# Joined 512-column matmuls in the Strassen-like gate/up products, taken apart into 256-column matmuls with one PSUM bank per product

## The chip, the cores and the metric

One core of one Trainium2 chip runs the whole kernel. The metric is the device time of one launch in microseconds (us), as the median of a few runs.

## The reference, cut to what matters

Two layers of an encoder block over 512 tokens of width 1024. The change touches only the gate and up products of the two feed-forward blocks of each layer (four in all):

```
def swiglu(x, w_gate, w_up, w_down):          # D_MODEL 1024, D_FF 2816, SEQ 512
    return (jax.nn.silu(x @ w_gate) * (x @ w_up)) @ w_down

for l in range(DEPTH):                         # DEPTH 2
    x = x + 0.5 * swiglu(rms_norm(x, ffn1_norm[l]), ...)
    ...                                        # attention and convolution, untouched
    x = x + 0.5 * swiglu(rms_norm(x, ffn2_norm[l]), ...)
    x = rms_norm(x, post_norm[l])
```

All of it is float32. The kernel reaches that accuracy by splitting each operand into a high part `hi` (rounded to the type fp32r) and a low part `lo` (what the rounding left), and by adding three matmuls: high weights by high data, high weights by low data, low weights by high data. The helper `mm3` issues these three, at L194, L195 and L196.

## The kernel before, in words

The 2816 hidden columns are worked in four chunks. The first chunk uses plain products on all 512 tokens (512-column matmuls through `mm3`). The other three chunks take two 128-column groups of gate and up together as a **pair** (nine pairs in each feed-forward, 36 in all) and use a Strassen-like scheme: features and tokens are cut in halves, and seven half-size products replace eight. A product works on 256 tokens (`HS`) and four 128x128 weight blocks for gate and four for up.

In the function `pair` the seven products run on TensorE in this order, kept by `order["pe"]`: b11, b21, t2, t3, t1, t4, b22. Four of them (b11, t2, t1, b22) go through `product`: 2 x 4 x 3 matmuls of 256 columns into one PSUM bank `bx`, gate in its left half and up in its right. Three (b21, t3, t4) go through `product_joined`: high and low data of a block lie side by side in one tile (`xj`, 512 columns), so that one 512-column matmul with the high weights does hi\*hi and hi\*lo at once (L418), and one 256-column matmul adds the low weights (L419):

```
T.matmul(o, w[0][:, c], both, start=start and k == 0, stop=False, skip_group_check=True)
last = T.matmul(o[:, 0:HS], w[1][:, c], both[:, 0:HS], start=False, stop=k == 3, ...).ins
```

A joined product therefore needs a bank for gate and one for up, each with the main sum on the left and the hi\*lo part on the right. VectorE (DVE) and ScalarE (ACT) add the two parts when they take the result out: `by` by two additions for each bank (L459, L460), `bz` after t3 by a copy for each bank (L428) and an addition of the halves (L470), `bz` after t4 by L477 and L478.

Weights come by DMA as float32 quarters (`fr`, `raw` tiles). DVE forms their sums for the scheme (L453 to L456), ACT casts the high part into a ring of four slots (`weights`, L284 and L442), and DVE subtracts for the low part (L286). For b21 and t4 the low part is made by an ACT pass (L434) and an accumulating DMA from GpSimd's queue into `ls` (L435). The slots lie at offsets `WOFF` and the tiles are padded by small gap tiles, so that the addresses of weights and data keep a fixed relation.

After a pair, `split` (L201, L202) makes high and low parts of its results. After the second and the third chunk `down` does the second matrix product in the same scheme, on 256-column matmuls through `mm3`, with the three pairs of the chunk as its inner dimension; its first products need the split results of the last pair. The order on each engine is fixed when the kernel is built: a scheduler places the instructions, bound by the `issue_after` rules in the code.

Of the kernel before, what the change touches and what calls it, by code (L numbers as in the profile page):

```python
# [62 lines left out]
WOP = 4  # L63
EVP = "DAD"
ORDER = "t0s1p3v4o5"
JOINED = ("b21", "t3", "t4")

VECS = [("g1", 8), ("gm", 8), ("g2", 8), ("gp", 8), ("gql", 3), ("gkl", 2),
        ("cw", 4 * CK), ("cb", 4), ("lg", 4), ("lb", 4), ("gq", 1), ("gk", 1), ("cp", PT)]
# [12 lines left out]
def encoder_kernel(ctx: ExitStack, tc: tile.TileContext, xT, consts, vecs, rgain, wgu1, wd1, wdq1,  # L82
# [210 lines left out]
    def ffn_body(fpool, l, gx, norm, wgu, wd, wdq, gain, done, w0, halved):  # L293
# [56 lines left out]

        def operands(R):

            def joined(src):
                both = fpool.tile([P, 2, S], FR, tag="xj", name=nm("xj"), bufs=WIDE)
                A.copy(both[:, :, 0:HS], src)
                V.tensor_tensor(both[:, :, HS:S], src, both[:, :, 0:HS].bitcast(FP), ALU.subtract)
                return both

            def halved(src, own=False):
                hi, lo = (fpool.tile([P, S], FR, tag="xs", name=nm("xs"), bufs=2) if own else slot(FR)  # L360
                          for _ in range(2))
                h3, l3 = (v.rearrange("p (j t) -> p j t", j=2) for v in (hi, lo))
                A.copy(h3, src)
                V.tensor_tensor(l3, src, h3.bitcast(FP), ALU.subtract)
                return hi, lo

            def diff(a, b, op=ALU.subtract):
                t = tmp().rearrange("p (j t) -> p j t", j=2)
                V.tensor_tensor(t, a, b, op)
                return t  # L370
            for i in range(2):
                e, o = wide(quarter()), wide(quarter())
                for j in range(2):
                    for par, t in ((0, e), (1, o)):
                        m = 4 * i + 2 * j + par
                        V.scalar_tensor_tensor(t[:, j], x[:, m, :], gain[:, m:m + 1], R, ALU.mult, ALU.mult)
                        yield
                b11, b12, b21, b22 = (v[:, :, h * HS:(h + 1) * HS] for v in (e, o) for h in range(2))
                for n, src in (("b11", b11), ("b21", b21)):
                    X[n].append((joined if n in JOINED else halved)(src))  # L380
                    yield
                t3 = diff(b12, b22)
                yield
                t2 = diff(t3, b11)
                yield
                X["t2"].append((joined if "t2" in JOINED else halved)(t2))
                yield
                X["t3"].append((joined if "t3" in JOINED else halved)(t3))
                yield
                t1 = diff(b11, b12)  # L390
                yield
                X["t1"].append((joined if "t1" in JOINED else halved)(t1))
                yield
                t4 = diff(b21, t2, ALU.add)
                yield
                X["t4"].append((joined if "t4" in JOINED else halved)(t4))
                yield
                X["b22"].append(halved(b22, i == 1))
                yield

        def product(o, w, n, start, stop):
# [6 lines left out]
                        last = mm3(o[:, gu * HS:(gu + 1) * HS], w[0][:, c], w[1][:, c], hi[:, t], lo[:, t],  # L408
                                   start and gu == 0 and k == 0, stop and k == 3, True)
            order["pe"] = last  # L410

        def product_joined(os, w, n, start):
            with tc.issue_after(order["pe"]):
                for gu, o in enumerate(os):
                    for k in range(4):
                        both = X[n][k // 2][:, k % 2]
                        c = slice(gu * 512 + k * P, gu * 512 + (k + 1) * P)
                        T.matmul(o, w[0][:, c], both, start=start and k == 0, stop=False, skip_group_check=True)  # L418
                        last = T.matmul(o[:, 0:HS], w[1][:, c], both[:, 0:HS], start=False, stop=k == 3,  # L419
                                        skip_group_check=True).ins  # L420
            order["pe"] = last

        def parts(os):

            return [(slice(gu * HS, (gu + 1) * HS), o[:, 0:HS], o[:, HS:S]) for gu, o in enumerate(os)]

        def copied(o, src):
            A.copy(o, src)  # L428
# [9 lines left out]
        def summed(w, src, n=WC, lo=None):  # L438

            lo = subtracted(w, src, n) if lo is None else lo  # L440
            hi = part(0, True)
            in_turn("h", lambda: A.copy(hi[:, :n], src[:, :n]))  # L442
            return hi, lo

        def pair(p, quartered):

            a11, a12, a21, a22, s3 = quarters(wgu[l, p], WC, p == CHUNKS[0][1])
            bx, by, bz = bank(), (bank(), bank()), (bank(), bank())
            product(bx, split_into("a11", a11), "b11", True, True)
            a = copied(tmp(), bx)  # L450
            product_joined(by, summed(wgu[l, p, 1], a12), "b21", True)
            with after("first"):
                V.tensor_tensor(s3, a11, a21, ALU.add)  # L453
                V.tensor_tensor(a21, a21, a22, ALU.add)
                V.tensor_tensor(a11, a11, a21, ALU.add)  # L455
                V.tensor_tensor(a12, a12, a11, ALU.add)  # L456
            s = tmp()
            for c, main, rest in parts(by):
                V.tensor_tensor(a[:, c], a[:, c], main, ALU.add)  # L459
                V.tensor_tensor(a[:, c], a[:, c], rest, ALU.add)  # L460
                if c.start == 0:
                    A.activation(s[:, 0:HS], a[:, 0:HS], AF.Silu)
            V.tensor_tensor(s[:, 0:HS], s[:, 0:HS], a[:, HS:S], ALU.mult)
            product(bx, split_into("s2", a11), "t2", False, True)
            r2 = wide(fpool.tile([P, WC], FP, tag="e", name=nm("e"), bufs=1))
            copied(r2[:, 0], bx)
            product_joined(bz, split_into("s3", s3), "t3", True)
            d = [copied(tmp(), o) for o in bz]
            for t in d:
                V.tensor_tensor(t[:, 0:HS], t[:, 0:HS], t[:, HS:S], ALU.add)  # L470
            product(bx, split_into("s1", a21), "t1", False, True)
            copied(r2[:, 1], bx)
            for t, (c, _, _) in zip(d, parts(bz)):
                order["first"] = V.tensor_tensor(r2[:, 1, c], t[:, 0:HS], r2[:, 1, c], ALU.subtract).ins
            product_joined(bz, summed(wgu[l, p, 3], a22), "t4", False)
            for c, main, rest in parts(bz):
                V.tensor_tensor(r2[:, 0, c], main, r2[:, 0, c], ALU.subtract)  # L477
                V.tensor_tensor(r2[:, 0, c], rest, r2[:, 0, c], ALU.add)  # L478
            s2 = tmp()
            s2v = s2.rearrange("p (h t) -> p h t", h=2)  # L480
            A.activation(s2v, r2[:, :, 0:HS], AF.Silu)
            V.tensor_tensor(s2v, s2v, r2[:, :, HS:S], ALU.mult)
# [12 lines left out]
            order["u0"] = V.tensor_tensor(u[:, h1], u[:, h0], s[:, h0], ALU.subtract).ins  # L495
            V.tensor_tensor(v[:, h0], s[:, h0], s[:, h1], ALU.subtract)
# [829 lines left out]
```

## Time and profile before

| what | before |
|---|---|
| median of 3 runs | 1773.75 us (1773.36 to 1775.32) |
| the profiled execution, its own time | 1775.6 us |
| its span, first to last instruction | 1773.8 us |
| TensorE (PE) busy, matmuls | 1757.2 us, 11430 |
| weight loads (PEld) busy | 1555.0 us, 11430 |
| DVE busy, instructions | 1488.6 us, 2309 |
| ACT busy, instructions | 1095.9 us, 1699 |
| GpSimd (POOL) busy | 381.3 us |
| mean granted TensorE clock | 1.000 |

PE is busy in 99% of the span, so what counts is how fast one matmul follows another. The durations of single matmuls overlap (they are pipelined); the distance from the start of one to the start of the next is read from the timeline, and is called the pace below. A pair takes about 19.5 us, the three pairs of the second feed-forward's third chunk run from 706 to 764.7 us of the span, and the `down` behind them from 764.7 to 794.7 us.

### The profile page before, as it was taken

To read this page: it belongs to the slowest core of one execution; us is meant where nothing else is said; L and a number is where in the kernel's file an instruction comes from. 1 tells how busy PE (TensorE), PEld (TensorE's weight loads), DVE (VectorE), ACT (ScalarE), POOL (GpSimd) and SP (SyncE) were. 2 spreads that over 40 slices of the span, in tenths; PEclk is the share of its full clock that TensorE was granted. 3 is DMA by queue.
4 is the path that set the end of the run, shared out by engine and by line. 5 is a ranking of instruction groups with operands and counts; after the bars stand their busy time and mean duration, and the time that the engine had idled before them with its cause. 6 is when DMAs were issued, how large, how long until landed. Compare 5 with 4: busy or idle time off the path is not lost. (4 is left out here: it accounts for less than half of the span.)

```text
span 1773.8 us, 29449 instructions
## 1 busy us (share of the span) xinstructions
PE 1757.2 (99%) x11430; PEld 1555.0 (88%) x11430; DVE 1488.6 (84%) x2309; ACT 1095.9 (62%) x1699; POOL 381.3 (21%) x315
## 2 busy tenths in 40 slices
PE   9999999999999999999999999999999999999998
PEld 7899999888678899999888999998986788999997
DVE  7899988688965999998779989885989568999883
ACT  5576766467953575756645757564778435767664
POOL 1001010248823000000310000002576410000001
PEclk9999999999999999999999999999999999999999
DMA  5567565324303466665326575743251126575742
GB/s 181 146 149 180 142 173 122 120 79 122 80 25 101 113 165 164 153 170 141 115 75 162 131 194 128 194 119 113 78 150 34 58 79 155 140 183 138 188 109 81
DMA packets 71947, 228.28 MB, mean 129 GB/s; under 512 B 8448, under 2 KB 9600, under 8 KB 71808
## 3 DMA queue, kind: packets, MB, share of 16 engines
q1 hardware_dynamic: 55536, 171.87, 30.7%
q0 software_dynamic: 16128, 54.53, 18.3%
q8 instruction: 89, 1.46, 0.3%
q14 instruction: 50, 0.41, 0.1%
q10 hardware_dynamic: 144, 0.00, 0.0%
HBM read 222.19 MB, written 2.10 MB: 126 GB/s over the span
## 5 line engine op out<-in xcount | busy, mean ns | idle before, releaser
L194 PE MATMUL ps<-r,weights 128*128 128x256 f32 (+1 forms) x2556 | 804.6, 318 | 2.8 <-ACT weights L1142 1.4
L195 PE MATMUL ps<-r,weights 128*128 128x256 f32 (+1 forms) x2556 | 804.4, 315 | 1.3 <-DVE r L202 1.3
L196 PE MATMUL ps<-r,weights 128*128 128x256 f32 (+1 forms) x2364 | 750.2, 319 | 3.2 <-DVE weights L162 2.3
L194 PEld LDWEIGHTS ps<-r,weights 128*128 128x128 f32 x2556 | 480.0, 188 | 50.2 <-ACT t L428 4.5
L195 PEld LDWEIGHTS ps<-r,weights 128*128 128x128 f32 x2556 | 480.6, 188 | 37.7 <-DVE r L202 2.8
L196 PEld LDWEIGHTS ps<-r,weights 128*128 128x128 f32 x2364 | 444.0, 188 | 39.4 <-DVE weights L162 3.6
L418 PE MATMUL ps<-xj,weights 128*128 128x512 f32 x864 | 306.4, 395 | 0.0
L155 ACT CAST weights<-raw 128x1024 fp32r<-128x1024 f32 (+3 forms) x148 | 131.7, 902 | 213.6 <-PE ps L195 120.7
L284 ACT CAST weights<-fr 128x1024 fp32r<-128x1024 f32 (+1 forms) x160 | 157.3, 983 | 100.3 <-DVE fr L455 51.8
L435 POOL DMA_DIRECT2D ls<-in_wgu x72 | 62.7, 871 | 724.9 <-ACT ls L434 664.3
L162 DVE TENSOR_TENSOR weights<-raw,weights 128x1024 fp32r<-128x1024 f32 (+3 forms) x132 | 142.8, 1090 | 81.0 <-ACT weights L155 79.9
L286 DVE TENSOR_TENSOR weights<-fr,weights 128x1024 fp32r<-128x1024 f32 (+1 forms) x160 | 182.3, 1139 | 21.3 <-ACT weights L284 21.3
L418 PEld LDWEIGHTS ps<-xj,weights 128*128 128x128 f32 x864 | 161.5, 188 | 31.0
L419 PE MATMUL ps<-xj,ls 128*128 128x256 f32 x576 | 162.5, 282 | 0.0
L1005 POOL TENSOR_TENSOR y<-y,pr 128x495 f32<-128x495 f32 (+29 forms) x90 | 118.8, 1323 | 46.2 <-ACT pr L1003 40.9
L284 ACT CAST weights<-raw 128x1024 fp32r<-128x1024 f32 (+1 forms) x100 | 97.8, 978 | 43.9 <-PE ps L195 22.9
L286 DVE TENSOR_TENSOR weights<-raw,weights 128x1024 fp32r<-128x1024 f32 (+1 forms) x100 | 113.5, 1135 | 11.4 <-ACT weights L284 10.9
L434 ACT ACTIVATE ls<-fr 128x1024 fp32r<-128x1024 f32 (+1 forms) x56 | 56.1, 1001 | 85.6 <-PE ps L419 46.1
L419 PEld LDWEIGHTS ps<-xj,ls 128*128 128x128 f32 x576 | 108.6, 189 | 0.0
L231 POOL TENSOR_TENSOR r<-r,t 128x512 f32<-128x512 f32 x45 | 74.0, 1654 | 132.2 <-ACT t L227 131.8
L999 DVE SCALAR_TENSOR_TENSOR cv<-m,vec,cv 128x511 f32<-128x511 f32 (+14 forms) x120 | 88.0, 733 | 4.0 <-ACT cv L995 2.4
L435 POOL DMA_DIRECT2D ls<-in_wdq x32 | 27.7, 865 | 258.2 <-ACT ls L434 258.2
(258 smaller groups left out, 2917.8 us busy)
## 6 DMA issues: line engine op xcount, KB each, us to landing
fr<-in_wgu SPq DMA_DIRECT2D x112, 512.0 KB, 4.2
ls<-in_wgu POOLq DMA_DIRECT2D x72, 512.0 KB, 7.2
raw<-in_wgu SPq DMA_DIRECT2D x62, 512.0 KB, 4.5
fr<-in_wdq SPq DMA_DIRECT2D x48, 384.0 KB, 4.5
ls<-in_wdq POOLq DMA_DIRECT2D x32, 384.0 KB, 4.9
raw<-in_wd SPq DMA_DIRECT2D x32, 384.0 KB, 3.2
raw<-in_wd SPq DMA_DIRECT2D x32, 256.0 KB, 2.8
raw<-in_wcv SPq DMA_DIRECT2D x16, 512.0 KB, 3.6
```

The lines of the kernel that those rows point to most:

```text
L155: order["cast"] = in_turn("h", lambda: A.copy(hi[:, :w], raw[:, :w]))
L162: in_turn(e, lambda: e.tensor_tensor(lo[:, :w], raw[:, :w], hi[:, :w].bitcast(FP), ALU.subtract))
L194: T.matmul(o, lh, rh, start=first, stop=False, skip_group_check=free)
L195: T.matmul(o, lh, rl, start=False, stop=False, skip_group_check=free)
L196: order["mm"] = T.matmul(o, ll, rh, start=False, stop=last, skip_group_check=free).ins
L284: in_turn("h", lambda: A.copy(hi[:, :w], src[:, :w]))
L286: order["lo"] = in_turn(V, lambda: V.tensor_tensor(lo[:, :w], src[:, :w], hi[:, :w].bitcast(FP), ALU.subtract))
L418: T.matmul(o, w[0][:, c], both, start=start and k == 0, stop=False, skip_group_check=True)
L419: last = T.matmul(o[:, 0:HS], w[1][:, c], both[:, 0:HS], start=False, stop=k == 3, skip_group_check=True).ins
L435: G.dma_start(out=lo[:, :n], in_=w, accum_op=ALU.add)
L999: V.scalar_tensor_tensor(acc[:, s:], u[c][:, :S - s], tap(k), acc[:, s:], ALU.mult, ALU.add)
L1005: order["conv"] = G.tensor_tensor(ys[c][:, s:], ys[c][:, s:], pr[:, s:], ALU.add).ins
```

## The change

`product_joined` and its helper `parts` go. All seven products now run through `product`: for each block hi\*hi, hi\*lo and lo\*hi, 256 columns each, into one bank. The tile `xj` stays where it was; its two halves now hold the high parts of two blocks and the low parts of the same two blocks. With one bank for each of b21 and t3/t4 a result is taken out by one instruction of 512 columns where there were two or four of 256.

```
-JOINED = ("b21", "t3", "t4")
+APART = ("b21", "t3", "t4")
...
-            def joined(src):
-                both = fpool.tile([P, 2, S], FR, tag="xj", name=nm("xj"), bufs=WIDE)
-                A.copy(both[:, :, 0:HS], src)
-                V.tensor_tensor(both[:, :, HS:S], src, both[:, :, 0:HS].bitcast(FP), ALU.subtract)
-                return both
...
+            def halved(src, where=""):
+                if where == "xj":
+                    both = fpool.tile([P, 2, S], FR, tag="xj", name=nm("xj"), bufs=WIDE)
+                    hi, lo = both[:, 0], both[:, 1]
...
-            bx, by, bz = bank(), (bank(), bank()), (bank(), bank())
+            bx, by, bz = bank(), bank(), bank()
...
-            product_joined(by, summed(wgu[l, p, 1], a12), "b21", True)
+            product(by, summed(wgu[l, p, 1], a12), "b21", True, True)
...
+            V.tensor_tensor(a, a, by, ALU.add)
             s = tmp()
-            for c, main, rest in parts(by):
-                V.tensor_tensor(a[:, c], a[:, c], main, ALU.add)
-                V.tensor_tensor(a[:, c], a[:, c], rest, ALU.add)
-                if c.start == 0:
-                    A.activation(s[:, 0:HS], a[:, 0:HS], AF.Silu)
+            A.activation(s[:, 0:HS], a[:, 0:HS], AF.Silu)
...
-            product_joined(bz, split_into("s3", s3), "t3", True)
-            d = [copied(tmp(), o) for o in bz]
-            for t in d:
-                V.tensor_tensor(t[:, 0:HS], t[:, 0:HS], t[:, HS:S], ALU.add)
+            product(bz, split_into("s3", s3), "t3", True, True)
+            d = copied(tmp(), bz)
...
-            for t, (c, _, _) in zip(d, parts(bz)):
-                order["first"] = V.tensor_tensor(r2[:, 1, c], t[:, 0:HS], r2[:, 1, c], ALU.subtract).ins
-            product_joined(bz, summed(wgu[l, p, 3], a22), "t4", False)
-            for c, main, rest in parts(bz):
-                V.tensor_tensor(r2[:, 0, c], main, r2[:, 0, c], ALU.subtract)
-                V.tensor_tensor(r2[:, 0, c], rest, r2[:, 0, c], ALU.add)
+            order["first"] = V.tensor_tensor(r2[:, 1], d, r2[:, 1], ALU.subtract).ins
+            product(bz, summed(wgu[l, p, 3], a22), "t4", False, True)
+            V.tensor_tensor(r2[:, 0], bz, r2[:, 0], ALU.subtract)
```

The changed file is shorter, so its lines have other numbers: what stood at L428, L434, L442, L453 to L456 stands 17 lines higher there (L411, L417, L425, L436 to L439), and what stood at L462, L481, L482, L484, L485, L490 to L497, L525, L536 and L537 stands 25 lines higher for L481 and behind it (L456, L457, L459, L460 and so on) and 20 higher for L462 (L442). L440 adds `by`, L451 and L453 are the two new subtractions. Lines up to L354 keep their numbers.

In the program as built GpSimd's and SyncE's instructions stand in the order of before, and TensorE's products do too. The scheduler moved instructions on DVE and ACT in the pairs. The first place is DVE from the end of t1 over the end of t4 into the next pair, in the first chunk of pairs; `ps` are PSUM banks, `e` holds the results of t1 and t2, `fr` and `raw` are weight quarters. Before:

```order
L477 TENSOR_TENSOR e_1027<-ps_940,e_1027 128x256
L474 TENSOR_TENSOR e_1027<-t_1047,e_1027 128x256
L474 TENSOR_TENSOR e_1027<-t_1049,e_1027 128x256
L453 TENSOR_TENSOR raw_1166<-fr_1158,fr_1160 128x1024
L478 TENSOR_TENSOR e_1027<-ps_940,e_1027 128x256
L477 TENSOR_TENSOR e_1027<-ps_941,e_1027 128x256
L454 TENSOR_TENSOR fr_1160<-fr_1160,fr_1161 128x1024
L478 TENSOR_TENSOR e_1027<-ps_941,e_1027 128x256
L455 TENSOR_TENSOR fr_1158<-fr_1158,fr_1160 128x1024
L485 TENSOR_TENSOR t_994<-t_994,ps_937 128x256
L482 TENSOR_TENSOR t_1106<-t_1106,e_1027 128x512
```

The same place in the changed kernel:

```order
L451 TENSOR_TENSOR e_1041<-t_1069,e_1041 128x512
L436 TENSOR_TENSOR raw_1188<-fr_1180,fr_1182 128x1024
L453 TENSOR_TENSOR e_1041<-ps_950,e_1041 128x512
L437 TENSOR_TENSOR fr_1182<-fr_1182,fr_1183 128x1024
L457 TENSOR_TENSOR t_1128<-t_1128,e_1041 128x512
L438 TENSOR_TENSOR fr_1180<-fr_1180,fr_1182 128x1024
L460 TENSOR_TENSOR t_1012<-t_1012,ps_948 128x256
L202 TENSOR_TENSOR r_1163<-t_1128,r_1162 128x512
```

Six small instructions became two, the product with Silu (L482, now L457) moved ahead of the weight sum for t2 (L455, now L438), and the low part of that result (L202) moved ahead of the last weight sum.

The second place is ACT over the same time, from the copy of t1's result to the copy of the next pair's b11 (`t_1198`, now `t_1218`), which frees the bank that t2 writes. Before:

```order
L428 COPY e_1027<-ps_937 128x512
L434 ACTIVATE ls_1312<-fr_1161 128x1024
L481 ACTIVATE t_1106<-e_1027 128x512
L484 ACTIVATE t_994<-ps_937 128x256
L284 CAST weights<-fr_1158 128x1024
L284 CAST weights<-raw_1166 128x1024
L284 CAST weights<-fr_1160 128x1024
L201 CAST r_1140<-t_1106 128x512
L428 COPY t_1198<-ps_1167 128x512
```

The same place in the changed kernel:

```order
L411 COPY e_1041<-ps_948 128x512
L417 ACTIVATE ls_1340<-fr_1183 128x1024
L456 ACTIVATE t_1128<-e_1041 128x512
L459 ACTIVATE t_1012<-ps_948 128x256
L201 CAST r_1162<-t_1128 128x512
L284 CAST weights<-fr_1180 128x1024
L284 CAST weights<-raw_1188 128x1024
L284 CAST weights<-fr_1182 128x1024
L411 COPY t_1218<-ps_1189 128x512
```

The cast L201 moved from behind the three weight casts to ahead of them; nothing stands any more between the last weight cast and the copy.

The third place is DVE from the last pair of that chunk into `down`, up to the low part of the pair's second result (L202). Before:

```order
L536 TENSOR_TENSOR fr_1390<-fr_1390,fr_1391 128x768
L478 TENSOR_TENSOR e_1257<-ps_1170,e_1257 128x256
L477 TENSOR_TENSOR e_1257<-ps_1171,e_1257 128x256
L537 TENSOR_TENSOR fr_1388<-fr_1388,fr_1390 128x768
L478 TENSOR_TENSOR e_1257<-ps_1171,e_1257 128x256
L485 TENSOR_TENSOR t_1224<-t_1224,ps_1167 128x256
L482 TENSOR_TENSOR t_1336<-t_1336,e_1257 128x512
L496 TENSOR_TENSOR t_1375<-t_1224 128x256
L286 TENSOR_TENSOR weights<-fr_1388,weights 128x768
L494 TENSOR_TENSOR u_1374<-t_1224,t_1336 128x256
L202 TENSOR_TENSOR r_1371<-t_1336,r_1370 128x512
```

The same place in the changed kernel:

```order
L511 TENSOR_TENSOR fr_1423<-fr_1423,fr_1424 128x768
L512 TENSOR_TENSOR fr_1421<-fr_1421,fr_1423 128x768
L453 TENSOR_TENSOR e_1282<-ps_1191,e_1282 128x512
L286 TENSOR_TENSOR weights<-fr_1421,weights 128x768
L457 TENSOR_TENSOR t_1369<-t_1369,e_1282 128x512
L460 TENSOR_TENSOR t_1253<-t_1253,ps_1189 128x256
L469 TENSOR_TENSOR u_1407<-t_1253,t_1369 128x256
L471 TENSOR_TENSOR t_1408<-t_1253 128x256
L202 TENSOR_TENSOR r_1404<-t_1369,r_1403 128x512
```

Both weight sums (L536, L537, now L511, L512) now stand ahead of the subtraction from t4's bank, and the low weights for t2 (L286) moved ahead of the product with Silu.

More of the change, by code (lines that the diff above doesn't have):

```diff
@@ L351, in operands @@
         def operands(R):
-            def joined(src):
-                both = fpool.tile([P, 2, S], FR, tag="xj", name=nm("xj"), bufs=WIDE)
-                A.copy(both[:, :, 0:HS], src)
-                V.tensor_tensor(both[:, :, HS:S], src, both[:, :, 0:HS].bitcast(FP), ALU.subtract)
-                return both
-            def halved(src, own=False):
-                hi, lo = (fpool.tile([P, S], FR, tag="xs", name=nm("xs"), bufs=2) if own else slot(FR)
-                          for _ in range(2))
+            def halved(src, where=""):
+                if where == "xj":
+                    both = fpool.tile([P, 2, S], FR, tag="xj", name=nm("xj"), bufs=WIDE)
+                    hi, lo = both[:, 0], both[:, 1]
+                else:
+                    hi, lo = (fpool.tile([P, S], FR, tag="xs", name=nm("xs"), bufs=2) if where else slot(FR)
+                              for _ in range(2))
                 h3, l3 = (v.rearrange("p (j t) -> p j t", j=2) for v in (hi, lo))
@@ L379, in operands @@
                 for n, src in (("b11", b11), ("b21", b21)):
-                    X[n].append((joined if n in JOINED else halved)(src))
+                    X[n].append(halved(src, "xj" if n in APART else ""))
                     yield
@@ L385, in operands @@
                 yield
-                X["t2"].append((joined if "t2" in JOINED else halved)(t2))
+                X["t2"].append(halved(t2))
                 yield
-                X["t3"].append((joined if "t3" in JOINED else halved)(t3))
+                X["t3"].append(halved(t3, "xj"))
                 yield
@@ L391, in operands @@
                 yield
-                X["t1"].append((joined if "t1" in JOINED else halved)(t1))
+                X["t1"].append(halved(t1))
                 yield
@@ L395, in operands @@
                 yield
-                X["t4"].append((joined if "t4" in JOINED else halved)(t4))
+                X["t4"].append(halved(t4, "xj"))
                 yield
-                X["b22"].append(halved(b22, i == 1))
+                X["b22"].append(halved(b22, "xs" if i else ""))
                 yield
@@ L410, in product @@
             order["pe"] = last
[L412 to L425, printed above, removed]
         def copied(o, src):
```

## The prediction

> **What bounds the kernel now.** I read the page first, then the groups kept apart by shape, then the timeline of TensorE through one pair, the waits, and the busy time by stretches.
>
> ```profile
> PE 1757.2 (99%) x11430; PEld 1555.0 (88%) x11430; DVE 1488.6 (84%) x2309; ACT 1095.9 (62%) x1699; POOL 381.3 (21%) x315
> L418 PE MATMUL ps<-xj,weights 128*128 128x512 f32 x864 | 306.4, 395 | 0.0
> L418 PEld LDWEIGHTS ps<-xj,weights 128*128 128x128 f32 x864 | 161.5, 188 | 31.0
> ```
>
> PE never rests for long, so the kernel is as fast as its matmuls follow each other, plus what PE waits. The change touches 864 places where a 512-column and a 256-column matmul become three of 256: 108 products of 8 blocks (36 pairs x 3). Every matmul has its weight load, so 864 matmuls and 864 loads are added.
>
> The durations overlap; the pace is read from the starts. The timeline of PE in a pair of the second feed-forward (its columns: start, us, engine, line):
>
> ```profile
> 736.80 0.28 PE L194 MATMUL ps<-r,weights 128*128 128x256 f32 x1
> ...
> 739.56 0.39 PE L418 MATMUL ps<-xj,weights 128*128 128x512 f32 x1
> ...
> 740.25 0.40 PE L418 MATMUL ps<-xj,weights 128*128 128x512 f32 x1
> 740.48 0.28 PE L419 MATMUL ps<-xj,ls 128*128 128x256 f32 x1
> 740.60 0.40 PE L418 MATMUL ps<-xj,weights 128*128 128x512 f32 x1
> ...
> 742.37 0.28 PE L194 MATMUL ps<-r,weights 128*128 128x256 f32 x1
> ...
> 743.08 0.28 PE L194 MATMUL ps<-xs,weights 128*128 128x256 f32 x1
> ...
> 744.44 0.28 PE L194 MATMUL ps<-xs,weights 128*128 128x256 f32 x1
> ...
> 745.12 0.28 PE L194 MATMUL ps<-r,weights 128*128 128x256 f32 x1
> ...
> 747.84 0.39 PE L418 MATMUL ps<-xj,weights 128*128 128x512 f32 x1
> ```
>
> These are the first matmuls of t1 (736.80), t4 (739.56, joined), b22 (742.37), the next pair's b11 (745.12) and b21 (747.84, joined). The joined product takes 742.37 - 739.56 = 2.81 us. b11, 24 matmuls of 256 columns, takes 747.84 - 745.12 = 2.72, or 0.1133 each, although it does the same arithmetic. t1 and b22, which follow a joined product, take 2.76 and 2.75. Inside the joined product a block costs 740.60 - 740.25 = 0.35, where three 256-column steps of b11 cost 0.34. b22's first six matmuls need 743.08 - 742.37 = 0.71 (0.118 each), its last six 745.12 - 744.44 = 0.68 (0.113 each): a slower pace is carried over from the joined product and dies out.
>
> Is 512 columns slow as such? In the mixing stage, a pure 512-column stream of 24 steps:
>
> ```profile
> 519.77 0.39 PE L194 MATMUL ps<-r,weights 128*128 128x512 f32 x1
> ...
> 525.21 0.39 PE L194 MATMUL ps<-r,weights 128*128 128x512 f32 x1
> ```
>
> 5.44 / 24 = 0.2267, exactly two paces of 0.1133. So neither width has a fixed cost; what costs is the alternation of the two widths, or something in the joined operands (a rival, below).
>
> **Part by part: TensorE's pace.** As pure 256-column streams the 108 products take 2.72 instead of 2.81 us: 108 x 0.09 = 9.7 us. The 108 products behind them lose their slow start, some 0.035 each: 3.8 us. Together 13.5 us, all on the path, since PE is the path. The bounds: at the top 14 us; at the bottom nothing or less, if the pace of the new streams is not b11's. The addresses speak for b11's: `xj` keeps its place, and `xs`, which lies behind it and is read in 256-column pieces, ran at 0.113 above.
>
> [...]
>
> **The added weight loads** I cost at nothing: in b11 24 loads, 188 ns each by the row above, pass within 2.72 us beside the matmuls. If they were not covered, 864 x 0.188 = 162 us would come on top.
>
> **DVE and ACT in the pair.** Rows by shape:
>
> ```profile
> L459 DVE TENSOR_TENSOR t<-t,ps 128x256 f32<-128x256 f32 x72 | 27.0, 414 | 0.1
> L470 DVE TENSOR_TENSOR t<-t 128x256 f32<-128x256 f32 x72 | 29.5, 419 | 2.3 <-ACT t L428 2.3
> L474 DVE TENSOR_TENSOR e<-t,e 128x256 f32<-128x256 f32 x72 | 27.7, 418 | 0.0
> L477 DVE TENSOR_TENSOR e<-ps,e 128x256 f32<-128x256 f32 x72 | 30.2, 420 | 31.3 <-PE ps L419 31.3
> L482 DVE TENSOR_TENSOR t<-t,e 128x512 f32<-128x512 f32 x36 | 24.7, 686 | 0.4
> L428 ACT COPY t<-ps 128x512 f32<-128x512 f32 x108 | 61.7, 579 | 2.4 <-PE ps L419 2.4
> ```
>
> In each pair twelve instructions of some 0.42 us (L459, L470, L474 and L477 by two, and L460 and L478, of the same shape as L459 and L477) become three of some 0.69: 5.0 - 2.1 = 2.9 us of DVE's time, and ACT loses one copy of 0.58. DVE is not the path as a whole, so this counts only where PE waits for it or for ACT:
>
> ```profile
> PEld ps L194 <- ACT t L428: 4.5, 24, 0.2
> PEld ps L195 <- DVE r L202: 2.8, 8, 0.4
> ```
>
> **The wait at t2.** 24 times (two pairs in each chunk) t2 waits for ACT to copy b11's bank. The rows for the pair above, ACT, DVE and PE:
>
> ```profile
> 740.60 0.58 ACT L428 COPY e<-ps 128x512 f32<-128x512 f32 x1
> 746.68 1.05 ACT L284 CAST weights<-fr 128x1024 fp32r<-128x1024 f32 x1 [0.97 <-DVE fr L455]
> 749.53 0.61 ACT L201 CAST r<-t 128x512 fp32r<-128x512 f32 x1
> 750.05 0.58 ACT L428 COPY t<-ps 128x512 f32<-128x512 f32 x1
> 745.43 1.21 DVE L455 TENSOR_TENSOR fr<-fr,fr 128x1024 f32<-128x1024 f32 x1
> 746.90 0.68 DVE L482 TENSOR_TENSOR t<-t,e 128x512 f32<-128x512 f32 x1
> 747.50 1.22 DVE L456 TENSOR_TENSOR raw<-raw,fr 128x1024 f32<-128x1024 f32 x1
> 748.63 0.42 DVE L496 TENSOR_TENSOR t<-t 128x256 f32<-128x256 f32 x1
> 749.31 1.22 DVE L286 TENSOR_TENSOR weights<-fr,weights 128x1024 fp32r<-128x1024 f32 x1
> 750.68 0.39 PE L194 MATMUL ps<-r,weights 128*128 128x256 f32 x1
> 750.90 0.28 PE L195 MATMUL ps<-r,weights 128*128 128x256 f32 x1
> ```
>
> The copy ends at 750.63 and t2 starts at 750.68, 0.03 late by 747.84 + 2.81, and its first step takes 0.22 in place of 0.11: 0.14 a time, 24 x 0.14 = 3.4 us. Now the cast L201 stands ahead of the three weight casts, so the copy follows the last of them, 750.05 - 749.53 = 0.52 earlier, if L438 (was L455) ends when it did. It does. On DVE a 512-column instruction is followed after 0.60 and a weight sum after 1.13 (747.50 - 746.90, 748.63 - 747.50). L451 can start at 741.18, when the copy of t1 ends; behind it and L436 the subtraction from t4's bank begins 1.73 later, 0.54 after t4's end at 742.37; L453, L437, L457 and L438 add 0.60 + 1.13 + 0.60 + 1.13: 4.0 after t4's end, against 4.27 before. PE will want the bank 3 x 2.72 = 8.16 after t4's end; the copy ends at 750.11 - 742.37 = 7.74. The wait goes, with 0.4 to spare. Late next are t2's low weights, L286, which ended at 750.53, 8.16 after t4's end, and are wanted 0.23 after t2 starts, at 8.39: 0.2 to spare. Bounds 0 and 3.4; I take 2.5.
>
> **The waits in `down`.** One stage by stretches (length, then busy PE, PEld, DVE, ACT, POOL), its start and where PE and DVE meet in it:
>
> ```profile
> 761.90 0.28 PE L194 MATMUL ps<-r,weights 128*128 128x256 f32 x1
> 764.70:794.70 30.00, 29.70 (x255) 29.04 (x254) 28.31 (x41) 17.03 (x22) 3.12 (x4) 1.00 0.72 187
> 768.06 0.28 PE L194 MATMUL ps<-r,weights 128*128 128x256 f32 x1
> 768.49 0.38 PE L195 MATMUL ps<-r,weights 128*128 128x256 f32 x1 [0.16 <-DVE r L202]
> 767.75 0.68 DVE L202 TENSOR_TENSOR r<-t,r 128x512 fp32r<-128x512 f32 x1
> ```
>
> 2 x 7 x 18 = 252 matmuls at 0.1133 are 28.56 us; the stage takes 30.00, so 1.44 are lost, and in 8 such stages 11.5. Nearly all lies in the first half, where DVE (28.31 busy of 30.00) makes the last pair's split results one after the other. The first of them, L202, ends at 768.43, which is 6.53 after t4's end (761.90, b22's first matmul); PE wants it 6.2 after (b22 2.72, b11 2.04, 13 matmuls of b21). In the new order fewer steps lie before it: L453 ends about 1.0 after t4's end; L457 waits for ACT's Silu and L286, to about 3.2; L460, L469, L471 and L202 bring it to about 5.0. Those behind (`u`, `v`) move up by about as much. Bounds 0 and 11.5; I take 6, since each step hangs on ACT between two of DVE and the second half's loss may stay.
>
> **The sum.** 13.5 + 2.5 + 6 = 22 us. Against the profiled execution, 1775.6 with a span of 1773.8, that is 1753.6; its time stands 1.85 above the median of the runs, 1773.75, so for a median I say 1752.
>
> **The rivals.** A measurement of this kernel can tell about 0.2%, 3.5 us, from no change.
>
> *Pace alone* (0.20): PE gets faster, but DVE and ACT are the next to be late, since PE now wants each result 0.3 to 0.5 earlier per pair. For it: DVE's 28.31 of 30.00 in `down`, and only 0.2 of spare time for L286 at t2. Against it: 2.9 us less work of DVE in each pair. Time: 1773.75 - 13.5 = 1760, and up to 1767 if a wait of 0.2 comes in each of the 36 pairs.
>
> *The joined operands are slow, not the alternation* (0.10, slower): every 256-column matmul that ran at 0.12 within a block read `xj`, so the new streams might stay there. 24 x 0.12 = 2.88 against 2.81, in 108 products +7.6 us: 1781, with the products behind them as slow as now. It decides from a pace of 2.81 / 24 = 0.117 on. Against it: b22's first six matmuls read `r` and are as slow, and the later ones speed up on the same tiles.
>
> *New waits outweigh the pace* (0.02, slower): over 0.13 per joined product.
>
> *Nothing to see* (0.03): pace and new waits cancel, 1774.
>
> [...]
>
> **How the numbers follow.** The forecast (pace and part of the waits, 1744 to 1760) has 0.64, so 1752. With all of the waits gone the sum is 13.5 + 3.4 + 11.5 = 28.4: 1745, and 1743 is the lower end. The upper end, 1768, takes in pace alone with new waits. Left out are the slower cases and little else. Faster 0.84, the same 0.03, slower 0.13.
>
> **What would show it.** In the new timeline t4 should take 2.72, as b11, and b22 behind it 2.72 from its first matmul on; three 256-column starts 0.34 apart in all seven products. The wait of PEld for ACT's copy should go from 24 to few, the one for L202 from 8 to few, and the first half of `down` should come near 14.3 us. Wrong would be starts 0.12 apart all through b21, t3 and t4, or new waits for L286 at t2.

## The result, and the profile after

| | before | after |
|---|---|---|
| median of 4 runs | 1774.35 us (1773.36 to 1775.32) | 1750.18 us (1749.53 to 1751.95) |
| span of the profiled execution | 1773.8 us | 1750.2 us |

The ratio is 0.9864, with a 95% interval of 0.9852 to 0.9876: 24 us faster, against 22 predicted (1752, range 1743 to 1768).

The first rows of the page, and TensorE's groups on `xj` (the high weights now take two lines, L194 and L195):

```profile
span 1750.2 us, 30816 instructions
PE 1735.9 (99%) x12294; PEld 1577.0 (90%) x12294; DVE 1411.2 (81%) x1985; ACT 1076.6 (62%) x1663; POOL 381.3 (22%) x315
L194 PE MATMUL ps<-xj,weights 128*128 128x256 f32 x864 | 238.5, 276 | 0.0
L195 PE MATMUL ps<-xj,weights 128*128 128x256 f32 x864 | 238.5, 276 | 0.0
L194 PEld LDWEIGHTS ps<-xj,weights 128*128 128x128 f32 x864 | 162.2, 188 | 0.0
```

PE has 864 matmuls more and is busy 21 us less. The timeline of PE in the same pair as before shows the first matmuls of t3, t1, t4 (with its first block), b22 (with its seventh matmul) and the next b11, and where t2 starts:

```profile
724.19 0.28 PE L194 MATMUL ps<-xj,weights 128*128 128x256 f32 x1
...
726.91 0.28 PE L194 MATMUL ps<-r,weights 128*128 128x256 f32 x1
...
729.63 0.28 PE L194 MATMUL ps<-xj,weights 128*128 128x256 f32 x1
729.74 0.28 PE L195 MATMUL ps<-xj,weights 128*128 128x256 f32 x1
729.86 0.28 PE L196 MATMUL ps<-xj,ls 128*128 128x256 f32 x1
729.97 0.28 PE L194 MATMUL ps<-xj,weights 128*128 128x256 f32 x1
...
732.35 0.28 PE L194 MATMUL ps<-r,weights 128*128 128x256 f32 x1
...
733.03 0.28 PE L194 MATMUL ps<-xs,weights 128*128 128x256 f32 x1
...
735.07 0.28 PE L194 MATMUL ps<-r,weights 128*128 128x256 f32 x1
...
740.40 0.28 PE L196 MATMUL ps<-xj,ls 128*128 128x256 f32 x1
740.51 0.28 PE L194 MATMUL ps<-r,weights 128*128 128x256 f32 x1
740.62 0.28 PE L195 MATMUL ps<-r,weights 128*128 128x256 f32 x1
```

Every product takes 2.72 us: t3, t1, t4 and b22. A block of t4 costs 729.97 - 729.63 = 0.34, b22's first six matmuls 733.03 - 732.35 = 0.68 (0.71 before). t2 starts 0.11 behind the last matmul of b21, and its second follows 0.11 later: its wait is gone in this pair. The list of waits, and the `down` stage (start of its first half, of its second, and of what follows; then busy times of the first half by stretches):

```profile
PEld ps L194 <- ACT t L411: 2.3, 8, 0.5
PEld ps L196 <- DVE weights L286: 1.1, 3, 0.5
754.11 0.28 PE L194 MATMUL ps<-r,weights 128*128 128x256 f32 x1
768.39 0.28 PE L194 MATMUL ps<-r,weights 128*128 128x256 f32 x1
782.81 0.28 PE L194 MATMUL ps<-r,weights 128*128 128x256 f32 x1
754.10:768.40 14.30, 14.30 (x129) 14.30 (x128) 13.89 (x23) 7.89 (x12) 0.86 (x1) 1.00 0.66 159
```

The first half takes 14.28 us, which is 126 matmuls at 0.1133 with nothing lost; the second 14.42. Together 28.70, where it was 30.00. The wait for ACT's copy is down from 24 times to 8, the one of L195 for L202 is off the list.

To set the parts of the time side by side I take the starts of all matmuls in pairs and `down` (four segments of the span), subtract 0.1133 for every 256 columns, and part what is left: small excess (under 0.014 per 256 columns) is **pace**, larger gaps are **stalls**. The ideal is 902 us in every kernel.

| kernel | pace loss, us | stalls in pairs, us | stalls in `down`, us |
|---|---|---|---|
| before | 13.7 | 3.9 | 12.1 |
| after | 0.6 | 3.4 | 1.8 |
| experiment 1 | 1.7 | 8.0 | 11.7 |
| experiment 2 | 13.4 | 1.0 | 6.2 |
| experiment 3 | 12.5 | 5.4 | 13.1 |
| experiment 4 | 48.0 | 0.0 | 0.0 |
| experiment 7 | 1.9 | 6.3 | 13.7 |
| experiment 11 | 0.4 | 0.7 | 1.2 |

Pace gave 13.1 us and stalls 10.8, nearly all of that in `down`: 23.9 us together, where the two spans differ by 23.6 and the medians by 24.2.

### The profile page after: what moved, and what is told of

Its sections match the earlier page's. It is cut to its first block, busy times and chain, and to the rows that moved or that the text cites. A ratio compares the mean times of both kernels' runs of the same rounds, so it can differ in the third digit from the quotient of the medians.

```text
span 1750.2 us, 30816 instructions
## 1 busy us (share of the span) xinstructions
PE 1735.9 (99%) x12294; PEld 1577.0 (90%) x12294; DVE 1411.2 (81%) x1985; ACT 1076.6 (62%) x1663; POOL 381.3 (22%) x315
## 5 line engine op out<-in xcount | busy, mean ns | idle before, releaser
L195 PE MATMUL ps<-r,weights 128*128 128x256 f32 (+1 forms) x2556 | 802.4, 314 | 0.0
L194 PE MATMUL ps<-r,weights 128*128 128x256 f32 (+1 forms) x2556 | 800.0, 316 | 1.5 <-ACT weights L1117 0.8
L194 PEld LDWEIGHTS ps<-r,weights 128*128 128x128 f32 x2556 | 480.0, 188 | 39.2 <-ACT t L411 2.3
L195 PEld LDWEIGHTS ps<-r,weights 128*128 128x128 f32 x2556 | 480.1, 188 | 35.0 <-issue 1.9
L194 PE MATMUL ps<-xj,weights 128*128 128x256 f32 x864 | 238.5, 276 | 0.0
L195 PE MATMUL ps<-xj,weights 128*128 128x256 f32 x864 | 238.5, 276 | 0.0
L286 DVE TENSOR_TENSOR weights<-fr,weights 128x1024 fp32r<-128x1024 f32 (+1 forms) x160 | 182.2, 1139 | 35.3 <-ACT weights L284 35.2
L195 PEld LDWEIGHTS ps<-xj,weights 128*128 128x128 f32 x864 | 162.2, 188 | 0.0
L194 PEld LDWEIGHTS ps<-xj,weights 128*128 128x128 f32 x864 | 162.2, 188 | 0.0
L286 DVE TENSOR_TENSOR weights<-raw,weights 128x1024 fp32r<-128x1024 f32 (+1 forms) x100 | 113.4, 1134 | 19.9 <-ACT weights L284 19.6
L417 ACT ACTIVATE ls<-fr 128x1024 fp32r<-128x1024 f32 (+1 forms) x56 | 56.1, 1002 | 88.8 <-PE ps L196 55.5
```

The lines of the kernel that those rows point to most:

```text
L194: T.matmul(o, lh, rh, start=first, stop=False, skip_group_check=free)
L195: T.matmul(o, lh, rl, start=False, stop=False, skip_group_check=free)
L286: order["lo"] = in_turn(V, lambda: V.tensor_tensor(lo[:, :w], src[:, :w], hi[:, :w].bitcast(FP), ALU.subtract))
L417: A.activation(lo[:, :n], src[:, :n], AF.Copy, scale=-1.0)
```

## The experiments

Two questions stood behind the prediction: are pace and waits really two separate gains, and is the slow pace a matter of alternating widths? Each time is given beside runs of the kernel before on the same chip (1773.4 to 1775.2).

**1. Pace without the new evacuation.** The kernel before, with each 512-column matmul cut into two of 256 into the same banks; DVE and ACT do what they did.

```diff
-T.matmul(o, w[0][:, c], both, ...)
+T.matmul(o[:, 0:HS], w[0][:, c], both[:, 0:HS], ...)
+T.matmul(o[:, HS:S], w[0][:, c], both[:, HS:S], ...)
```

> The kernel before, with each joined 512-column matmul cut into two of 256 columns on the same tiles and into the same banks (hi*hi left, hi*lo right); all of DVE's and ACT's evacuation stays as before. Theory A (alternating widths slow the pace; the evacuation work makes the waits): b21, t3 and t4 take 2.72 us instead of 2.81, t1 and b22 2.72 instead of 2.76, the waits at t2 and in `down` stay (about 1.3 us in the first half of each `down`); 1759 to 1764 us. Rival B (the joined operands are slow, not the alternation): products stay at 2.81 to 2.88, 1774 to 1781. Rival C (the whole gain is DVE's relief): 1774.

Measured: 1767.05 us, ratio 0.9952 (0.9936 to 0.9968), 3 us above the range expected. The pace loss went from 13.7 to 1.7, but stalls in the pairs grew from 3.9 to 8.0. Its waits:

```profile
PEld ps L194 <- ACT t L431: 5.8, 24, 0.2
PEld ps L195 <- DVE r L202: 2.8, 8, 0.4
```

The copy of b11's bank is as late as before and PE comes to t2 earlier, so the wait grows from 4.5 to 5.8 on the same 24 places. The pace is a gain of its own, and some 4 of its 12 us are given back where DVE and ACT aren't relieved. The 864 added loads show no cost here either: with them the pace loss falls to 1.7. The two banks of a joined product are still in use at that pace, so they aren't what made it slow.

**2. Less DVE without the new pace.** The kernel before, without the six additions that bring in the hi\*lo part of b21, t3 and t4 (L460, L470 and L478, two each); its output lacks these terms.

```diff
-V.tensor_tensor(a[:, c], a[:, c], rest, ALU.add)
...
-for t in d:
-    V.tensor_tensor(t[:, 0:HS], t[:, 0:HS], t[:, HS:S], ALU.add)
...
-V.tensor_tensor(r2[:, 0, c], rest, r2[:, 0, c], ALU.add)
```

> The kernel before with the joined matmuls as they are, but six of the twelve small DVE instructions of a pair are left out (the additions of the hi*lo parts: L460 by two, L470 by two, L478 by two), so the output misses the hi*lo terms of b21, t3 and t4. Theory A: joined products stay at 2.81 and the ones behind them at 2.76, most of the loss in the first half of `down` goes (it was 1.3 us in each of 8 stages); 1762 to 1768 us. Rival C (the whole gain is DVE's relief): about 1751. Rival D (the waits go because PE's pace is uniform, not because of DVE): 1773.

Measured: 1766.28 us, ratio 0.9950 (0.9935 to 0.9965). The pace stays (13.4), stalls fall from 16.0 to 7.3. The largest wait for another engine that is left, and where one of its nine stands, in the row of PE:

```profile
PEld ps L196 <- DVE weights L286: 5.3, 9, 0.6
768.42 0.39 PE L196 MATMUL ps<-r,weights 128*128 128x256 f32 x1 [0.43 <-DVE weights L286]
```

The waits for L428 and L202 are off the list, and the low weights are the next to be late, eight times of nine in `down`. So the two gains can be had apart. With fewer instructions the scheduler's order on DVE and ACT changed here too.

**3. No alternation inside a product.** The kernel before, with the eight 512-column matmuls of a joined product first and the eight of 256 behind them.

```diff
+for wide_step in (True, False):
     for gu, o in enumerate(os):
         for k in range(4):
...
+            if wide_step: T.matmul(o, w[0][:, c], both, ...)
+            else: last = T.matmul(o[:, 0:HS], w[1][:, c], both[:, 0:HS], ...).ins
```

> The kernel before, with the sixteen matmuls of a joined product in another order: the eight of 512 columns first, then the eight of 256. Same operands, addresses, banks and number of instructions. Theory A (alternation): steps near 0.227 and 0.113 but for a change-over, a joined product 2.72 to 2.76; 1760 to 1766 us. Rival B1 (512 columns against weights at the shifted offset are slow): the 512s stay at 0.233, the 256s go to 0.113, 2.77 a product; 1768 to 1771. Rival B2 (the joined operands or the two banks are slow): 2.81, 1774.

Measured: 1775.03 us, ratio 1.0003 (0.9994 to 1.0013): nothing. The scheduler kept eight and eight in 76 of the 108 products and made it two groups of each in the others. The timeline of PE over one of the 76 (each of the first two rows holds eight matmuls):

```profile
728.19 2.02 PE L420 MATMUL ps<-xj,weights 128*128 128x512 f32 x8
730.04 1.10 PE L422 MATMUL ps<-xj,ls 128*128 128x256 f32 x8
730.98 0.28 PE L194 MATMUL ps<-r,weights 128*128 128x256 f32 x1
```

Eight 512s need 1.85 us, 0.231 each, in a run of their own width, where the mixing stage's 512s take 0.2267; the eight 256s behind them 0.94, 0.1175 each. The alternation isn't the cause. Something in the operands makes these 512s slow, and the slow pace goes on behind them: through the 256s and, though the last of these (730.87 to 730.98) is back at 0.11, through the first seven steps of the next product, at 0.116 to 0.122.

**4. Other places for the weights.** Weights read by 256-column products lie in slots shifted by 16 or 48 columns (64 or 192 bytes, `WOFF`), those of the plain 512-column products in unshifted ones. Here the changed kernel with no shift; the tile keeps its width, so that nothing else moves.

```diff
-WOFF = 16, 48
+WOFF = 0, 0
```

> The changed kernel with the shifted weight slots (16 and 48 columns) put at offset 0; every other tile stays where it was. If a uniform width alone gives 0.1133 a matmul (theory A in its plain form), nothing changes: 1749 to 1752 us. If the relation of weight and data addresses sets the pace too, the 8064 matmuls of 256 columns in pairs and `down` go towards 0.12: up to 8064 x 0.0065 = 52 us more, 1800.

Measured: 1794.21 us, ratio 1.0107 (1.0092 to 1.0122), 44 us above the changed kernel. The timeline of PE, from the first matmul of t2 to the first of t3 and of t1:

```profile
717.49 0.28 PE L194 MATMUL ps<-r,weights 128*128 128x256 f32 x1
717.61 0.28 PE L195 MATMUL ps<-r,weights 128*128 128x256 f32 x1
...
720.37 0.28 PE L194 MATMUL ps<-xj,weights 128*128 128x256 f32 x1
...
723.25 0.28 PE L194 MATMUL ps<-r,weights 128*128 128x256 f32 x1
```

2.88 us a product, 0.120 a matmul, on `r` as on `xj`. The only thing that changed is where the weights lie. Products with low weights in `ls`, which did not move, show 0.119, 0.121 and 0.113 in turn.

**5. The mirror.** The changed kernel, with the plain 512-column products' weights in shifted slots as well.

```diff
-hi = part(0)
+hi = part(0, True)
...
-lo = low()
+lo = low(True)
...
```

> The changed kernel, with the weights of the plain 512-column products also put into the shifted slots (16 and 48 columns) that the 256-column products use; data tiles stay. Theory A2 (formed after the grouped run: a 512-column matmul is slow when its weights are shifted against its data, whatever stands beside it): the pure 512-column streams go from 0.2267 to about 0.232 a matmul; some 2500 of them, 1760 to 1766 us. Theory A (alternation of widths): no change, 1749 to 1752.

Measured: 1760.97 us, ratio 0.9924 (0.9909 to 0.9938), 11 us above the changed kernel. The first matmuls of two 512-column products, 24 steps apart:

```profile
42.21 0.39 PE L194 MATMUL ps<-r,weights 128*128 128x512 f32 x1
...
47.78 0.39 PE L194 MATMUL ps<-r,weights 128*128 128x512 f32 x1
```

5.57 / 24 = 0.232, where it was 5.44 / 24 = 0.2267. The two widths want opposite places: 512 columns the unshifted slots (0.2267 against 0.232), 256 the shifted ones (0.1133 against 0.120). The joined 512s of the kernel before read shifted slots.

**6. Moving `xj` alone by 64 bytes**, in the kernel before, to give its 512s the distance from their weights that the plain ones have.

```diff
-fpool.tile([P, 2, S], FR, tag="xj", name=nm("xj"), bufs=WIDE)
 fpool.tile([P, S], FR, tag="xs", name=nm("xs"), bufs=2)
-fpool.tile([P, 48], FP, tag="gap", name=nm("gap"), bufs=1)
+fpool.tile([P, 16], FP, tag="gap", name=nm("gap"), bufs=1)
+fpool.tile([P, 2, S], FR, tag="xj", name=nm("xj"), bufs=WIDE)
+fpool.tile([P, 32], FP, tag="gapb", name=nm("gapb"), bufs=1)
```

> The kernel before, joined, with only the tile xj moved by 64 bytes (its neighbours keep their places), so that the 512-column matmuls see their shifted weights as the plain ones see theirs. Theory A2: the 512s go from 0.232 to 0.227, the 256s to 0.113 if their new distance to the low weights is as good as the old, a joined product 2.72 to 2.77, with the waits as in the run of three 256s: 1765 to 1770 us. Theory A (alternation): a joined product stays at 2.81, 1774.

Measured: 1773.29 us, ratio 0.9997 (0.9987 to 1.0006); t4 takes 2.78 us instead of 2.81. The distance of a matmul's own weights and data is not enough.

**7. DVE's work given back.** The changed kernel, with four maxima of a tile with itself per pair (512 columns, 2.4 us of DVE).

```diff
+V.tensor_tensor(a, a, a, ALU.max)
...
+for _ in range(2):
+    V.tensor_tensor(d, d, d, ALU.max)
...
+V.tensor_tensor(r2[:, 0], r2[:, 0], r2[:, 0], ALU.max)
```

> The changed kernel with four added DVE instructions of 512 columns in each pair, maxima of a tile with itself beside the three new evacuations: 2.4 of the 2.9 us that the change took from DVE come back, TensorE's work is untouched. If the waits went because DVE has less to do: they come back, 6 to 10 us, 1756 to 1761. If the new order did it: 1750 to 1753.

Measured: 1767.70 us, ratio 0.9962 (0.9949 to 0.9975). The pace loss stays small (1.9), stalls rise from 5.2 to 20.0, above the 16.0 of the kernel before. Its waits:

```profile
PEld ps L195 <- DVE r L202: 5.7, 8, 0.7
PEld ps L194 <- ACT t L411: 3.7, 15, 0.3
```

Both old waits are back, and the rise is larger than either case forecast. So the stalls hang on DVE, but perhaps not on its work alone: the added instructions also changed the scheduler's order on DVE and ACT, and this run doesn't part the two.

**8. Both shifts at 32 columns** (128 bytes), in the changed kernel; the tile of the weights keeps its width.

```diff
-WOFF = 16, 48
+WOFF = 32, 32
```

> The changed kernel with both shifts of the weight slots at 32 columns in place of 16 and 48. The distances 64 and 192 bytes gave 0.1133, distance 0 gave 0.12. If any distance that is not 0 is good: 0.1133, 1749 to 1752 us. [...]

Measured: 1790.38 us, ratio 1.0091 (1.0074 to 1.0108); 2.85 to 2.88 us a product again, 2.80 with `ls`. It isn't whether there is a shift: with 64 and 192 bytes a product of 256 columns takes 2.72, with 0 (experiment 4) 2.83 to 2.88, with 128 2.80 to 2.88.

**9. Moving only `ls` by 192 bytes**, in the kernel before. b21 and t4 read it, t3 doesn't.

```diff
-fpool.tile([P, 48], FP, tag="gap", name=nm("gap"), bufs=1)
 fpool.tile([P, WC], FR, tag="ls", name=nm("ls"), bufs=2)
+fpool.tile([P, 48], FP, tag="gap", name=nm("gap"), bufs=1)
```

> The kernel before, joined, with only the tile ls (low weights of b21 and t4) moved by 192 bytes, so that low weights and xj have distance 0; t3, whose low weights lie elsewhere, is the control. If the pace of a matmul goes with the weights that are loaded while it runs (a 512 wants distance 0 there, a 256 wants 64 or 192): b21 and t4 fall to 2.72, t3 stays at 2.81. If it goes with its own weights: the 256s of b21 and t4 get slower, 2.81 to 2.85. If the alternation does it: 2.81 all three.

Measured: 1772.91 us, one run, against 1775.16. The timeline of PE: t3, t1 and t4 of one pair, by their first matmuls, and t4's first two blocks:

```profile
751.18 0.62 PE L418 MATMUL ps<-xj,weights 128*128 128x512 f32 x2
...
753.96 0.28 PE L194 MATMUL ps<-r,weights 128*128 128x256 f32 x1
...
756.72 0.39 PE L418 MATMUL ps<-xj,weights 128*128 128x512 f32 x1
756.94 0.28 PE L419 MATMUL ps<-xj,ls 128*128 128x256 f32 x1
757.06 0.39 PE L418 MATMUL ps<-xj,weights 128*128 128x512 f32 x1
...
759.44 0.28 PE L194 MATMUL ps<-r,weights 128*128 128x256 f32 x1
```

t4 takes 2.72 us with the two widths in turn; t3, the control in the same pair, 2.78, and t1 behind t3 2.76. In every pair t3 takes what it took in the kernel before, 2.78 or 2.81. This settles the prediction's cause: alternating 512 and 256 columns costs nothing in t4 as it lies here, 2.72 us as in a stream of 256 alone. The whole run gains little, since `down`'s product with `ls` gets slower (2.11 us against 2.04) and the wait at t2, where ACT's copy comes no earlier and PE does, grows from 4.5 to this:

```profile
PEld ps L194 <- ACT t L428: 9.1, 24, 0.9
```

**10. `xj` and `ls` both moved by 64 bytes**, in the kernel before, so that each 512 stands to its own weights as the plain ones do.

```diff
-fpool.tile([P, 2, S], FR, tag="xj", name=nm("xj"), bufs=WIDE)
 fpool.tile([P, S], FR, tag="xs", name=nm("xs"), bufs=2)
-fpool.tile([P, 48], FP, tag="gap", name=nm("gap"), bufs=1)
+fpool.tile([P, 16], FP, tag="gap", name=nm("gap"), bufs=1)
+fpool.tile([P, 2, S], FR, tag="xj", name=nm("xj"), bufs=WIDE)
+fpool.tile([P, 48], FP, tag="gapb", name=nm("gapb"), bufs=1)
 fpool.tile([P, WC], FR, tag="ls", name=nm("ls"), bufs=2)
```

> The kernel before, joined, with xj and ls both moved by 64 bytes: in b21 and t4 the 512s see their own weights at distance 0 and the 256s theirs at 192, the two distances that were fast in pure streams; t3 keeps low weights at 128. If the pace goes with a matmul's own weights: b21 and t4 fall to 2.72, t3 to 2.77. If the alternation of widths costs by itself: b21 and t4 stay at 2.77 or more.

Measured: 1775.71 us, one run; t4 2.81 us, steps of about 0.233, 0.113, 0.233 and 0.121 in turn; t3 2.78 or 2.79, as in experiment 6. A miss for the idea of own weights by distance. Modulo 128 bytes the weights lie as in experiment 9, and only the data's place differs: it matters too, 2.81 us for t4 against 2.72.

**11. One step further.** Most of the stalls left in the pairs of the changed kernel stood behind ACT's copies (L411). Here t1's result is subtracted straight from its bank and the copy goes.

```diff
-copied(r2[:, 1], bx)
-order["first"] = V.tensor_tensor(r2[:, 1], d, r2[:, 1], ALU.subtract).ins
+order["first"] = V.tensor_tensor(r2[:, 1], d, bx, ALU.subtract).ins
```

> The changed kernel with t1's result taken out by DVE's subtraction straight from the bank, without ACT's copy before it: one ACT instruction of 0.58 us less in each pair, and DVE can start 1.5 us earlier after t1. If the waits that are left (5.2 us in pairs and `down` together) come from late DVE and ACT work: 1746 to 1749 us. If they are waits for data or the bank: 1750, the same.

Measured: 1748.26 us (1747.88 to 1750.36), ratio 0.9847 (0.9834 to 0.9860). Stalls fall from 5.2 to 1.9 in the profile and the wait for L411 leaves the list. It beats the kernel before; that it beats the changed one isn't shown, as the two intervals overlap.

**12. The data moved instead of the weights.** Experiment 4, with 16 columns more behind the weight buffer: `xj`, `xs` and `ls` move by 64 bytes, `weights` and `r` stay.

```diff
-weights = wpool.tile([P, 2 * WN * WC + 48], FR, name="weights", bufs=1)
+weights = wpool.tile([P, 2 * WN * WC + 64], FR, name="weights", bufs=1)
```

> The variant with both shifts at 0, and beside it 16 columns behind the weight buffer, which move `xj`, `xs` and `ls` by 64 bytes; `weights` and `r` stay. If the distance between weights and data decides, the products on `xj` (now 64 bytes from the weights modulo 128) run at 2.72 to 2.76 us (0.113 a matmul, after a slow start of some seven matmuls behind a product on `r`), while those on `r` stay at 2.88; the time is some 12 us under that variant's 1794, about 1782. If the weights' own address decides, or anything else than the distance, all stay at 0.120, 2.88 us a product, and the time at 1794.

Measured: 1794.87 us, one run. The timeline of PE from the first matmul of t3 to the first of t1:

```profile
720.59 0.28 PE L194 MATMUL ps<-xj,weights 128*128 128x256 f32 x1
...
723.42 0.29 PE L194 MATMUL ps<-r,weights 128*128 128x256 f32 x1
```

2.83 us, 0.118 a matmul: a little under 2.88, far from 2.72. The distance alone doesn't decide either; a theory that had fitted experiments 4, 5 and 8 fell.

## Why the prediction was right, and where it was wrong

**The pace: 13.5 us predicted, 13.1 measured.** Products of 2.72, followers at full pace from their first matmul, three starts 0.34 apart: as written. A cost of 0.09 per joined product and 0.035 per follower, read from starts, carried to every pair. Most of the difference is t3, which the sum held at 2.81: before, it took 2.78 in 17 of the 36 pairs.

**Its cause was wrong.** The prediction put the slow pace down to "the alternation of the two widths, or something in the joined operands (a rival, below)". Experiments 3 and 9 throw out the first. The operands' places were the cause: experiment 9 moves the low weights alone and brings t4 to full pace. How they act stays open: the joined 512s read weights from slots in which a pure stream of 512 columns is slow (0.232, experiment 5), but in experiment 9 they still do, and run at 0.227. The error did no harm here, because 256-column matmuls run at 0.1133 from those slots; the rival's sign (1781) was wrong because it held `xj` to be slow for 256 columns, and `xj` ran at 0.113. Had the weights of these products lain as in experiment 4, where t4 takes 2.83 us and t3 2.88, they would have cost 72 x 0.11 + 36 x 0.16 = 13.7 us more (an estimate), the whole gain in pace. Experiments 4 and 8 move the weights of all 256-column products, and stand 42 and 38 us above the forecast. The sentence "The addresses speak for b11's" was the step that carried the result.

**The added loads: nothing, as costed.** The groups show 864 loads of `weights` at 188 ns on each of L194 and L195, and t4's 24 loads (4.5 us of load time) lie within 2.72. In t4's first block they begin at 729.52, 729.63 and 729.75, each with the matmul before its own (729.52, 729.63, 729.74). No fixed part per matmul shows either: the steps are in proportion to the columns, 2.72 / 24 = 0.1133 us for 256 and 5.44 / 24 = 0.2267 for 512. Of the prediction's 0.13 for slower, 0.01 was for loads that are not covered, 162 us; the trace shows nothing of it.

**The wait at t2: 2.5 us predicted.** In the pair of the timeline it went as worked out. The rows of DVE and ACT there:

```profile
739.29 1.21 DVE L286 TENSOR_TENSOR weights<-fr,weights 128x1024 fp32r<-128x1024 f32 x1
739.58 0.57 ACT L411 COPY t<-ps 128x512 f32<-128x512 f32 x1
```

Counted from t4's end (732.35) the copy ends at 7.80 (7.74 predicted), the low weights at 8.15 (8.16), and PE starts t2 at 8.16. But stalls inside the pairs fell only from 3.9 to 3.4 us over all four segments: the 24 small waits for the copy gave way to 8 larger ones, 0.2 to 0.5 us, in two pairs of each segment. So this term came to 0.5, not 2.5.

**The waits in `down`: 6 us predicted, 10.3 measured** (12.1 to 1.8). The prediction's working was right in its times, and its size was a choice between bounds 0 and 11.5. The row of the first low part (DVE) in the same `down`:

```profile
755.86 0.68 DVE L202 TENSOR_TENSOR r<-t,r 128x512 fp32r<-128x512 f32 x1
```

It ends at 756.54, and t4's end is at 751.39 (one pair, 7 x 2.72 = 19.04, behind the 732.35 above): 5.15 after it, where 5.0 was worked out, 6.53 stood before, and PE wants it at 6.2. With 1.0 us to spare this wait is gone, and so are those behind it in that half. The mis-sized step is the halving "since each step hangs on ACT between two of DVE": ACT was 7.89 busy of 14.30 in that half and had room. The second half's loss did stay, but it is 0.14 us of the 1.44.

The term for t2 was 2.0 us too high and the one for `down` 4.3 too low. That the sum, 22 us, came as near to 23.9 as it did is partly luck.

**The rivals.** Pace alone (1760 to 1767) is experiment 1 almost to the letter, 1767, with the waits grown; it didn't happen because the same change relieved DVE and ACT and gave them another order (experiment 7 doesn't part these two). L286 at t2, the mechanism feared, ends no wait at t2 of a pair: its three waits, 1.1 us in all, stand in one b11 and in two `down` stages.

## What to carry to other kernels

A pace that is off by a few per cent (here 2.81 us a product against 2.72) and dies out over the next matmuls (here 0.118 for six of them, then 0.113) may come from the operands' places: regroup the stream and move one tile by 64 bytes before blaming the shape. When a width changes, ask which addresses were laid out for which width. And a gain in pace may pay in full only if what evacuates the banks gets faster with it, as 4 of the 12 us in experiment 1 show; where bounds for a wait are wide, compare when the result comes and when it is wanted, and take the bound that this comparison points to.

## What the runs showed of the hardware

In these runs the pace of a stream of matmuls depends on where weights and data lie: moves by 64 bytes change it (from 0.1133 to 0.120 for 256 columns, by experiment 4), and smaller ones were not tried. In bytes within a partition modulo 128, by the addresses of the programs as built, for streams of one width:

| columns | weights | data | pace per matmul, us | from |
|---|---|---|---|---|
| 256 | 0 | 64 | 0.1133 | after |
| 256 | 64 | 64 | 0.119 to 0.120 | experiments 4, 8 |
| 256 | 64 | 0 | 0.118 | experiment 12 |
| 512 | 64 | 64 | 0.2267 | before, after |
| 512 | 0 | 64 | 0.231 to 0.232 | experiments 3, 5 |

The weight buffer begins at 64, so that a shift of 64 or 192 bytes puts weights at 0 (0.1133), one of 0 or 128 at 64 (0.119 to 0.120). With data at 64 the weights' place decides, and the two widths want opposite ones, 5.9% apart for 256 columns and 2.4% for 512. The place modulo 128 isn't everything: experiments 4 and 8 agree in it, and t4 takes 2.83 us in one and 2.80 in the other. In mixed streams it isn't that simple: in experiment 9 the 512s' own weights lie at 0 and the 256s' at 64, both wrong by the table, and both run at full pace (2.72 us for t4). There each matmul has the place that suits its width in the weights whose load begins with it (a 512 starts at 747.42, and so does the load for the 256 behind it). That reading fits the alternating streams with data at 64, if a slow pace is carried over to some seven matmuls (experiment 3 shows seven at 0.116 to 0.122), and the total of experiment 4's triples. It doesn't fit which of the three is the quick one, nor experiment 3, where the next product begins slowly after the last of the 256s was quick again, nor the data at 0 (experiment 10). Why the places matter stays open.
